# Row-tiled gate matmuls in a hybrid mLSTM / RG-LRU layer: 64x64 blocks on the two row halves of the array

## The chip, the cores and the metric

The kernel runs on one core of a Trainium2 chip. The metric is the device time of one launch in microseconds. Before the change three runs gave 1915.2, 1918.41 and 1918.58 us; their median is 1918.41 us.

## The reference, cut to what matters

The program is one layer of a diffusion backbone over 1024 latent tokens and 256 context tokens of width 2048. A modulated RMS norm feeds one wide input projection (2048 to 6160 columns). Its outputs go to two mixers: an mLSTM with 4 heads, scanned in chunks in both directions, and an RG-LRU of 1024 channels, scanned token by token in both directions. The context's final states seed the scans over the latent tokens. Both mixers' gated outputs are joined and go through an output projection (2048 to 2048), a residual and a last norm.

The RG-LRU gates are the subject here. The 1024 channels form 16 blocks of 64, and each block has its own 64x64 matrix, for two directions and two gates (r and i):

```python
xb = xc.reshape(bsz, t, R_BLOCKS, R_BLOCK)
r  = sigmoid(einsum('btgi,gij->btgj', xb, w_r).reshape(bsz, t, ch) + b_r)
ii = sigmoid(einsum('btgi,gij->btgj', xb, w_i).reshape(bsz, t, ch) + b_i)
log_a = -LRU_C * r * softplus(-lam)
a = exp(log_a)
u = sqrt(-expm1(2.0 * log_a)) * (ii * xc)      # h[t] = a[t] * h[t-1] + u[t], both directions
```

## The kernel before

All large products run in float32r, with each operand split into a high and a low part, so that a product is three matmuls (high x high, high x low, low x high). Weights come through a ring of three buffers: ScalarE copies a piece to its high part `whi` (L209), VectorE subtracts to get the low part `wlo` (L210).

The work has five stages: phase A (modulation, norm and transposes), the context projections, the heads of x with the mLSTM scans beside them, the RG phase, and the output projection. A small clock in the program (`Clock`) decides where the work of the mixers is emitted among the projections' matmuls: each mixer is a generator that sleeps for so many microseconds of projection work. The tile framework then fixes one order for each engine and waits by semaphore where data or a buffer demands it. Within an engine the order is kept.

The RG-LRU handles 128 channels at a time, "tile 0" to "tile 7", each holding two 64-channel blocks. `rg_gen` does one such tile: a convolution (POOL L663, VectorE L665), then `gate_mm`, the gate matmuls, the sigmoids (L858), the products and activations (L871 to L875), two scans (L882) and, for x, the output gate (L896). It runs twice for each tile:

- over the 256 context tokens (`ctx_rg_all`), beside the heads of x. Here the gate matmul is one plain float32 matmul (L916).
- over the 1024 latent tokens (`x_rg`), in the RG phase, beside the projections of the next tiles (`ct_unit`, lines L1176, L1179, L1182; one unit is 96 matmuls into one `mm` buffer). Here the gate matmul is the triple L1294, L1295, L1296, with xc split into `xs` (ScalarE, L1288) and `xl` (VectorE, L1289).

The two 64x64 blocks of a tile lie on the diagonal of a 128x128 matrix whose other half is zero: `load_wrg` puts them there, and the zeros are set once with a memset. For each of the 4 pairs (direction, gate) and each half of the tokens, one PSUM bank of the pool `mx` (4 banks, shared with the scans and the transposes) takes the result of 128 channels by 512 tokens, and one sigmoid of 128x512 reads it.

At the end of the RG phase stands the join with the output projection (`out_unit`, L1397 to L1399): its first block needs the two `mm` buffers, the second of which is read by the evacuation of the last z unit (ScalarE L1379, VectorE L1380). ScalarE also splits the stored outputs of the mixers there (`y_split`, L1362).

Of the kernel before, what the change touches and what calls it, by code (L numbers as in the profile page):

```python
# [9 lines left out]
F32 = mybir.dt.float32  # L10
F32R = mybir.dt.float32r
# [41 lines left out]
class Clock:  # L53
    """Emission order of the parts: each generator yields how long (in us of TensorE work) it sleeps."""
# [50 lines left out]
class Slots:  # L105
    """Counts the live tiles of one tag, so that no tile is taken before its slot's last use is emitted."""
# [26 lines left out]
class Ring:  # L133
    """Weights: loaded, split into two float32r parts, ahead of their use."""
# [14 lines left out]
    def add(self, n, cols, loads, per, dest=None):  # L149
        """n k-tiles of cols columns; loads: (first column, source [128, n, c]); per: k-tiles per piece."""  # L150
# [79 lines left out]
def tile_hymba(ctx: ExitStack, tc: tile.TileContext, x, c, cx, c_ctx, w_mod, b_mod, norm_g, w_in, b_gate,  # L230
# [63 lines left out]
    negS = const.tile([128, 16], F32, name="negS")  # L294
    hafS = const.tile([128, 16], F32, name="hafS")
# [96 lines left out]
    def wm_fill(limit=4 * KT):  # L392
        """loads of the modulation weights, as far ahead as there is room"""
# [54 lines left out]
    def mv_fin(k):  # L448
        """scale and shift columns of k-tile k: scale x, scale ctx, shift x, shift ctx"""
# [24 lines left out]
    DVE.tensor_copy(out=cols, in_=pt[:, 0:184])  # L474
    DVE.tensor_scalar(out=b1sc, in0=cols[:, cSC:cSC + 16], scalar1=1.0, scalar2=None, op0=ADD)
# [18 lines left out]
    def mv_some(n, limit):  # L494
        """the next n pieces of the modulation products"""
# [16 lines left out]
    def log1p_exp_neg(z, den, t, t2):  # L512
        """z = e^-|a| -> t(z) with log(1 + z) = 2 t(z)."""
# [10 lines left out]
    # 8 softplus(-lambda)  # L524
# [11 lines left out]
    # row norms  # L536
# [29 lines left out]
    def main_a(k, q):  # L566
        """a quarter of the products of k-tile k"""
# [17 lines left out]
    def to_hx(k, src, s, oh, ol, w, v):  # L585
        """float32r parts of scale * src + shift"""
# [56 lines left out]
    def j2r(ap):  # L643
        """[128, 1024] in raster order, seen in column-major order"""
# [16 lines left out]
    def conv(xp, cv, T, wb, bb, ct):  # L661
        """causal-style 4-tap convolution of a channel tile; xp holds T + 3 columns"""
# [862 lines left out]
```

## Time and profile before

| | |
|---|---|
| runs | 1915.2, 1918.41, 1918.58 us (median 1918.41) |
| profiled execution | span 1915.9 us from the first to the last instruction; no other time of it is given, and the span lies within the runs |
| TensorE | busy 1821.8 us, 95% |
| VectorE, ScalarE, GpSimdE | busy 930.5, 808.8 and 327.8 us |
| x gates of the RG-LRU | 192 matmuls of 512 columns, 64 sigmoids of 128x512 |
| context gates | 32 float32 matmuls of 256 columns (64 in the trace), 32 sigmoids of 128x256 |
| RG phase, first gate matmul to last sigmoid | 1194.3 to 1549.7 us |

A busy time of TensorE is not its cost in a stream: matmuls overlap in the pipeline, so that the distance from one start to the next is what each takes from the engine, and the duration (about 390 ns for 512 columns) is longer than that.

### The profile page before, as it was taken

The numbers are of one execution on the slowest core, as the hardware profiler recorded it, in microseconds if no ns is written. First come the engines' busy times: TensorE is split into PE (matmuls) and PEld (weight loads), VectorE is DVE, ScalarE is ACT, GpSimd is POOL, SyncE is SP. The second block draws the span as 40 slices with busy tenths as digits, with TensorE's granted clock in tenths as the row PEclk, the third lists the DMA queues.
The fourth block names the chain that finished last, engine by engine and source line by source line (L and its number), as shares of the span: only waits on it lengthen the run. The fifth ranks groups of instructions, "written<-read, shape, count | busy, mean of one in ns | idle before, by whom it ended". The sixth has DMA issues, their size and how long they took to land.

```text
span 1915.9 us, 24921 instructions
## 1 busy us (share of the span) xinstructions
PE 1821.8 (95%) x9489; PEld 1499.0 (78%) x9489; DVE 930.5 (49%) x1580; ACT 808.8 (42%) x1228; POOL 327.8 (17%) x414
## 2 busy tenths in 40 slices
PE   1888999999999999999999999999999989999998
PEld 0455999888898878988798878778878877888786
DVE  5776654435543552134322444777755655434432
ACT  4444553335745531133312431755555664324322
POOL 2420001012101210012000210221221223222221
PEclk9999999999999999999999999999999999999999
DMA  9996676223222132112221214344332236446533
GB/s 272 284 291 180 184 189 161 69 56 67 66 78 53 47 72 67 45 46 65 58 67 48 55 45 133 118 124 133 115 102 58 77 123 201 154 123 229 168 113 132
DMA packets 293927, 223.50 MB, mean 117 GB/s; under 512 B 25792, under 2 KB 256408, under 8 KB 293808
## 3 DMA queue, kind: packets, MB, share of 16 engines
q1 hardware_dynamic: 285688, 198.64, 37.9%
q10 hardware_dynamic: 5336, 14.36, 2.0%
q0 software_dynamic: 2784, 8.92, 1.3%
q8 instruction: 75, 1.23, 0.3%
q14 instruction: 44, 0.36, 0.1%
HBM read 202.39 MB, written 19.48 MB: 116 GB/s over the span
## 4 chain that ended last, share of the span: by engine, by line
PE 70%; DMA 9%; DVE 8%; issue 5%; ACT 4%; POOL 2%; SPq 2%; ACTq 0%; DVEq 0%; POOLq 0%
PE mm L1182 11%; PE mm L1176 11%; PE mm L1179 11%; PE mm L1219 2%; PE mm L1221 2%; PE mm L1222 2%; DMA gw<-in_w_mod_dram 2%; DMA wm<-in_w_mod_dram 2%; PE mm L1397 2%; PE mm L1398 2%; PE mm L1399 2%; PE mx L1398 2%; PE mx L1399 2%; PE mx L1397 2%; DMA yst<-yD 1%
## 5 line engine op out<-in xcount | busy, mean ns | idle before, releaser
L210 DVE TENSOR_TENSOR wlo<-raw,whi 128x512 fp32r<-128x512 f32 (+1 forms) x392 | 294.9, 761 | 562.0 <-ACT whi L209 561.4
L209 ACT ACTIVATE whi<-raw 128x512 fp32r<-128x512 f32 (+1 forms) x392 | 242.6, 628 | 559.3 <-PE mm L1179 259.0
L1176 PE MATMUL mm<-hxh,whi 128*128 128x512 f32 x1216 | 396.9, 407 | 0.3 <-DVE Gx L1208 0.3
L1182 PE MATMUL mm<-hxh,wlo 128*128 128x512 f32 x1216 | 384.4, 397 | 0.0
L1179 PE MATMUL mm<-hxl,whi 128*128 128x512 f32 x1216 | 382.6, 395 | 0.0
L1179 PEld LDWEIGHTS mm<-hxl,whi 128*128 128x128 f32 x1216 | 229.2, 188 | 54.4
L1182 PEld LDWEIGHTS mm<-hxh,wlo 128*128 128x128 f32 x1216 | 229.8, 189 | 53.3
L1176 PEld LDWEIGHTS mm<-hxh,whi 128*128 128x128 f32 x1216 | 227.6, 189 | 52.5 <-issue 1.9
L1219 PE MATMUL mm<-whi,hxh 128*128 128x256 f32 x384 | 109.8, 286 | 0.4 <-DVE s L1257 0.2
L1221 PE MATMUL mm<-wlo,hxh 128*128 128x256 f32 x384 | 108.1, 282 | 0.0
L1222 PE MATMUL mm<-whi,hxl 128*128 128x256 f32 x384 | 107.5, 281 | 0.0
L1397 PE MATMUL mm<-whi,hxh 128*128 128x512 f32 x256 | 101.8, 398 | 5.0 <-DVE s L1380 5.0
L1398 PE MATMUL mm<-wlo,hxh 128*128 128x512 f32 x256 | 101.4, 396 | 0.0
L1399 PE MATMUL mm<-whi,hxl 128*128 128x512 f32 x256 | 101.4, 396 | 0.0
L1398 PE MATMUL mx<-wlo,hxh 128*128 128x512 f32 x192 | 75.8, 395 | 2.0 <-DVE wlo L210 2.0
L1397 PE MATMUL mx<-whi,hxh 128*128 128x512 f32 x192 | 75.9, 395 | 1.7 <-ACT whi L209 1.6
L433 PE MATMUL mx<-wm,silP 128*32 128x256 f32 x512 | 43.2, 426 | 35.1 <-DMA wm<-in_w_mod_dram 30.1
L1399 PE MATMUL mx<-whi,hxl 128*128 128x512 f32 x192 | 75.5, 393 | 0.0
L1219 PEld LDWEIGHTS mm<-whi,hxh 128*128 128x128 f32 x384 | 72.5, 189 | 1.2 <-issue 0.5
L1314 DVE SCALAR_TENSOR_TENSOR ga<-gw,silc,ga 128x512 f32<-128x512 f32 x60 | 55.2, 920 | 36.4 <-DMA gw<-in_w_mod_dram 35.9
L1221 PEld LDWEIGHTS mm<-wlo,hxh 128*128 128x128 f32 x384 | 72.4, 188 | 0.3
L1222 PEld LDWEIGHTS mm<-whi,hxl 128*128 128x128 f32 x384 | 72.2, 189 | 0.0
(323 smaller groups left out, 3180.3 us busy)
## 6 DMA issues: line engine op xcount, KB each, us to landing
raw<-in_w_in_dram SPq DMA_DIRECT2D x136, 512.0 KB, 4.0
wm<-in_w_mod_dram SPq DMA_DIRECT2D x128, 256.0 KB, 5.6
raw<-in_w_out_dram SPq DMA_DIRECT2D x64, 512.0 KB, 4.8
gw<-in_w_mod_dram SPq DMA_DIRECT2D x64, 256.0 KB, 2.8
X<-in_x_dram SPq DMA_DIRECT2D x16, 512.0 KB, 7.6
NI<-niD SPq DMA_DIRECT2D x64, 128.0 KB, 4.5
xpc<-in_x_dram SPq DMA_DIRECT2D x32, 256.0 KB, 3.5
yD<-s ACTq DMA_DIRECT2D x15, 512.0 KB, 2.8
```

The lines of the kernel that those rows point to most:

```text
L209: self.nc.scalar.activation(out=hi, in_=src, func=AF.Copy)
L210: self.nc.vector.tensor_tensor(out=lo, in0=src, in1=hi.bitcast(F32), op=SUB)
L1176: PE.matmul(out=ps[:, ts], lhsT=hi, rhs=hxh[k][:, ts], start=(k == 0), stop=False)
L1179: PE.matmul(out=ps[:, ts], lhsT=hi, rhs=hxl[k][:, ts], start=False, stop=False)
L1182: PE.matmul(out=ps[:, ts], lhsT=lo, rhs=hxh[k][:, ts], start=False, stop=(k == KT - 1))
L1219: PE.matmul(out=o, lhsT=hxh[k][:, sl], rhs=hi, start=(k == 0 and tt % 2 == 0), stop=False, skip_group_check=True)
L1221: PE.matmul(out=o, lhsT=hxh[k][:, sl], rhs=lo, start=False, stop=False, skip_group_check=True)
L1222: PE.matmul(out=o, lhsT=hxl[k][:, sl], rhs=hi, start=False, stop=(k == KT - 1), skip_group_check=True)
L1314: DVE.scalar_tensor_tensor(out=a, in0=t, scalar=silc[:, k:k + 1], in1=a, op0=MUL, op1=ADD)
L1397: PE.matmul(out=pst[jt], lhsT=hxh[j][:, sl], rhs=hi, start=(j == 0), stop=False)
L1398: PE.matmul(out=pst[jt], lhsT=hxh[j][:, sl], rhs=lo, start=False, stop=False)
L1399: PE.matmul(out=pst[jt], lhsT=hxl[j][:, sl], rhs=hi, start=False, stop=(j == KT - 1))
```

## The change

The zeros are left out. The weight tile holds, for each channel of a block, the 4 x 64 columns (direction, gate, output channel), so that 128 columns of it are the r gate and the i gate of one direction. A matmul takes the 64 rows of one block and gives 128 outputs: r on partitions 0 to 63, i on partitions 64 to 127. The two blocks b of a tile stand on the two row halves of the array (`tile_position=(64 * b, 0)`), each with a PSUM bank of its own. So the number of gate matmuls is as before: 2 blocks instead of 2 gates.

A sigmoid now reads 64 partitions (one gate of one block) and writes 64 partitions, with its bias from a new small tile `brg` that four VectorE copies fill at the start. There are twice as many sigmoids. All matmuls of one direction are emitted at one point (12 for x, 2 for the context), the sigmoids behind them, and then one sleep of 3.6 us (0.9 for the context) stands in the place of the sleeps of 0.9 us after each sigmoid. The slots of both gates are taken at the start of a direction. The split of the weights (L1283, L1284) shrinks from 128x512 to 128x256, and two memsets go.

```diff
-            SP.dma_start(out=t[64 * g:64 * g + 64, :, 64 * g:64 * g + 64], in_=src)
+            SP.dma_start(out=t[64 * g:64 * g + 64, :, :], in_=src)
...
         for d in range(2):
-            for g in range(2):
-                t = yield from S.get()
-                (rt if g == 0 else it)[d] = t
-                for h0 in range(0, T, wd):
-                    ps = mx_tile()
-                    pre_g(ps[:, 0:wd], 2 * d + g, slice(h0, h0 + wd))
-                    act(out=t[:, h0:h0 + wd], in_=ps[:, 0:wd], func=AF.Sigmoid, bias=col(cBR, 8 * (2 * d + g) + i))
-                    yield 0.9
+            rt[d] = yield from S.get()
+            it[d] = yield from S.get()
+            parts = []
+            for h0 in range(0, T, wd):
+                two = [mx_tile()[:, 0:wd] for _ in range(2)]
+                pre_g(two, d, slice(h0, h0 + wd))
+                parts.append((h0, two))
+            for h0, two in parts:
+                for b in range(2):
+                    for g, t in enumerate((rt[d], it[d])):
+                        act(out=t[64 * b:64 * b + 64, h0:h0 + wd], in_=two[b][64 * g:64 * g + 64, :], func=AF.Sigmoid,
+                            bias=brg[64 * g:64 * g + 64, b, d, i:i + 1])
+            yield 3.6 * sc
...
-            def f(ps, dg, ts):
-                PE.matmul(out=ps, lhsT=W[:, dg, :], rhs=xc[:, ts], start=True, stop=True)
+            def f(two, d, ts):
+                for b, ps in enumerate(two):
+                    r = slice(64 * b, 64 * b + 64)
+                    PE.matmul(out=ps, lhsT=W[r, 2 * d:2 * d + 2, :].rearrange("p a b -> p (a b)"), rhs=xc[r, ts],
+                              start=True, stop=True, tile_position=(64 * b, 0))
...
-                PE.matmul(out=ps, lhsT=hl[:, 0, cs], rhs=xs[:, ts], start=True, stop=False)
-                PE.matmul(out=ps, lhsT=hl[:, 0, cs], rhs=xl[:, ts], start=False, stop=False)
-                PE.matmul(out=ps, lhsT=hl[:, 1, cs], rhs=xs[:, ts], start=False, stop=True)
+                for w, src in ((0, xs), (0, xl), (1, xs)):
+                    for b, ps in enumerate(two):
+                        r = slice(64 * b, 64 * b + 64)
+                        PE.matmul(out=ps, lhsT=hl[r, w, cs], rhs=src[r, ts], start=(src is xs and w == 0),
+                                  stop=(w == 1), tile_position=(64 * b, 0))
```

On TensorE, tile 4 of the RG phase shows the form that tiles 3 to 7 have. Before, the first triples stand among the projection's matmuls (`mm`), one PSUM bank (`mx`) each:

```order
L1294 MATMUL mx_11706<-s_11671,s_11616 128x512
L1295 MATMUL mx_11706<-s_11672,s_11616 128x512
L1296 MATMUL mx_11706<-s_11671,s_11616 128x512
L1176 MATMUL mm_11600<-hxh_1258,whi_11601 128x512 x2
L1179 MATMUL mm_11600<-hxl_1257,whi_11601 128x512 x2
L1182 MATMUL mm_11600<-hxh_1258,wlo_11602 128x512 x2
L1294 MATMUL mx_11718<-s_11671,s_11616 128x512
L1295 MATMUL mx_11718<-s_11672,s_11616 128x512
L1296 MATMUL mx_11718<-s_11671,s_11616 128x512
```

After, the same place holds one direction's 12 gate matmuls in a row (11768 and 11769 are the banks of the two blocks for the first 512 tokens, 11776 and 11777 for the others; 11738 and 11739 are `xs` and `xl`):

```order
L1308 MATMUL mx_11768<-s_11738,s_11680 128x512
L1308 MATMUL mx_11769<-s_11738,s_11680 128x512
L1308 MATMUL mx_11768<-s_11739,s_11680 128x512
L1308 MATMUL mx_11769<-s_11739,s_11680 128x512
L1308 MATMUL mx_11768<-s_11738,s_11680 128x512
L1308 MATMUL mx_11769<-s_11738,s_11680 128x512
L1308 MATMUL mx_11776<-s_11738,s_11680 128x512
L1308 MATMUL mx_11777<-s_11738,s_11680 128x512
L1308 MATMUL mx_11776<-s_11739,s_11680 128x512
L1308 MATMUL mx_11777<-s_11739,s_11680 128x512
L1308 MATMUL mx_11776<-s_11738,s_11680 128x512
L1308 MATMUL mx_11777<-s_11738,s_11680 128x512
```

The two halves of the array take turns there; 18 projection matmuls follow, then the 12 of the second direction. Before, a tile's eight triples were eight visits among 42 projection matmuls.

In tiles 0, 1 and 2 the second direction comes out differently on TensorE after the change (here tile 0; 10505 to 10514 are the four banks):

```order
L1308 MATMUL mx_10505<-s_10421,s_10358 128x512
L1308 MATMUL mx_10505<-s_10422,s_10358 128x512
L1308 MATMUL mx_10505<-s_10421,s_10358 128x512
L1188 MATMUL mm_10543<-hxh_529,whi_10411 128x512 x2
L1191 MATMUL mm_10543<-hxl_528,whi_10411 128x512
L1308 MATMUL mx_10506<-s_10421,s_10358 128x512
L1308 MATMUL mx_10506<-s_10422,s_10358 128x512
L1308 MATMUL mx_10506<-s_10421,s_10358 128x512
```

The three steps of one block run behind one another on one half, with projection matmuls before the other block's three. So over the eight tiles the 192 gate matmuls form 78 neighbours on opposite halves and 36 that stand alone, in 28 groups between projection matmuls; the context's 32 form 15 neighbours and 2 alone, in 14 groups.

On ScalarE, the last tile (7) and the join. Before, the last z unit's evacuation (L1379, into 12620) stands here among the sigmoids and the splits of the stored outputs (`yst`):

```order
L1362 ACTIVATE hxh_995<-yst_8_12824 128x512
L1362 ACTIVATE hxh_1083<-yst_9_12828 128x512
L858 ACTIVATE s_12797<-mx_12798,cols 128x512
L209 ACTIVATE whi_12818<-raw_12589 128x512
L1379 ACTIVATE s_12620<-mm_12621 128x64x16
L858 ACTIVATE s_12797<-mx_12809,cols 128x512
```

After, it is L1392, behind all 16 sigmoids of the tile and the same two splits:

```order
L867 ACTIVATE s_12887<-mx_12896,brg 64x512
L209 ACTIVATE whi_12928<-raw_12681 128x512
L867 ACTIVATE s_12886<-mx_12897,brg 64x512
L867 ACTIVATE s_12887<-mx_12897,brg 64x512
L1375 ACTIVATE hxh_1000<-yst_8_12934 128x512
L1375 ACTIVATE hxh_1088<-yst_9_12938 128x512
L1392 ACTIVATE s_12711<-mm_12712 128x64x16
```

What moved with it on TensorE: before, 6 matmuls of the output projection and 2 of the gates stood between the last z unit and the first use of the second `mm` buffer; after, 18 of the output projection do.

## Rows read from the trace of the kernel before

**Rows 1.** The page: busy time of each engine, share of the span, instructions.

```profile
PE 1821.8 (95%) x9489; PEld 1499.0 (78%) x9489; DVE 930.5 (49%) x1580; ACT 808.8 (42%) x1228; POOL 327.8 (17%) x414
```

**Rows 2.** Busy time by stretch: RG phase, context gates (clock and DMA last).

```profile
1194.30:1549.70 355.40, 344.19 (x1450) 275.18 (x1451) 235.18 (x221) 217.85 (x244) 82.93 (x55) 0.99 0.35 105
441.50:633.50 192.00, 191.22 (x1038) 165.00 (x1037) 85.60 (x208) 112.29 (x181) 30.02 (x67) 1.00 0.26 65
```

**Rows 3.** Timeline, TensorE: start, duration, line; gate triple, float32 matmuls of 257 columns.

```profile
1372.80 0.40 PE L1294 MATMUL mx<-s,s 128*128 128x512 f32 x1
1373.03 0.39 PE L1295 MATMUL mx<-s,s 128*128 128x512 f32 x1
...
440.04 0.60 PE L1112 MATMUL mx<-s,KW 128*128 128x257 f32 x2
...
440.48 0.60 PE L1107 MATMUL mx<-s,SP 128*128 128x257 f32 x2
```

**Rows 4.** Timeline, TensorE: modulation matmuls on four column tiles between full-array matmuls.

```profile
95.01 0.50 PE L580 MATMUL mm<-hxh,wlo 128*128 128x512 f32 x1
95.44 0.64 PE L433 MATMUL mx<-wm,silP 128*32 128x256 f32 x8
96.01 0.50 PE L577 MATMUL mm<-hxh,whi 128*128 128x512 f32 x1
...
113.22 1.07 PE L433 MATMUL mx<-wm,silP 128*32 128x256 f32 x16 [0.98 <-DVE ft L590]
```

**Rows 5.** Two stretches of 30 ns, line L433 alone (PE and PEld, count in brackets).

```profile
94.46:94.49 0.03, 0.03 (x4) 0.03 (x8) 1.00 1.22 307
94.70:94.73 0.03, 0.03 (x8) 0.00 (x0) 1.00 1.14 290
```

**Rows 6.** Timeline: matmuls of 256 columns and their weight loads (PEld).

```profile
985.03 0.28 PE L1221 MATMUL mm<-wlo,hxh 128*128 128x256 f32 x1
985.03 0.19 PEld L1222 LDWEIGHTS mm<-whi,hxl 128*128 128x128 f32 x1
985.15 0.28 PE L1222 MATMUL mm<-whi,hxl 128*128 128x256 f32 x1
```

**Rows 7.** Timeline and lines, ScalarE: sigmoids, a 64-partition copy, table loads.

```profile
1196.54 3.00 ACT L858 ACTIVATE s<-mx,cols 128x512 f32<-128x512 f32 x5 [2.22 <-PE mx L1296]
1201.20 1.85 ACT L858 ACTIVATE s<-mx,cols 128x512 f32<-128x512 f32 x3
...
L719 ACT ACTIVATE s<-mx 64x512 f32<-64x512 f32 x6 | 3.2, 588 | 3.1 <-PE mx L716 3.0
L858 ACT ACT_TABLE_LOAD x20 | 25.7, 1283 | 2.6 <-DVE gb L1323 2.2
```

**Rows 8.** Waits of TensorE from 1180 to 1620: total us, times, longest.

```profile
PE mm L1397 <- DVE s L1380: 5.0, 1, 5.0
PE mx L1294 <- ACT s L1288: 3.1, 3, 1.9
```

**Rows 9.** Timeline around tile 1: TensorE, and ScalarE's store of tile 0's output.

```profile
1236.04 0.80 PE L1294 MATMUL mx<-s,s 128*128 128x512 f32 x1 [2.08 <-ACT s L858]
1236.63 0.63 PE L1295 MATMUL mx<-s,s 128*128 128x512 f32 x1
1237.05 0.63 PE L1296 MATMUL mx<-s,s 128*128 128x512 f32 x1
...
1232.72 0.33 ACTq L904 DMA_DIRECT2D yD<-s  x1
```

**Rows 10.** The join: TensorE, ScalarE, and the stretch behind it.

```profile
1544.30 0.77 PE L1397 MATMUL mm<-whi,hxh 128*128 128x512 f32 x1 [4.96 <-DVE s L1380]
...
1537.97 1.25 ACT L1362 ACTIVATE hxh<-yst 128x512 fp32r<-128x512 f32 x2 [2.81 <-DMA yst<-yD]
1540.22 1.89 ACT L1379 ACTIVATE s<-mm 128x1024 f32<-128x1024 f32 x1
...
1545.00:1550.00 5.00, 5.00 (x14) 3.85 (x13) 1.03 (x2) 2.24 (x4) 1.38 (x3) 0.50 0.34 112
```

More of the change, by code (lines that the diff above doesn't have):

```diff
@@ L294, in tile_hymba @@
     negS = const.tile([128, 16], F32, name="negS")
+    brg = const.tile([128, 2, 2, 8], F32, name="brg")
     hafS = const.tile([128, 16], F32, name="hafS")
@@ L474, in tile_hymba @@
     DVE.tensor_copy(out=cols, in_=pt[:, 0:184])
+    for g in range(2):
+        for b in range(2):
+            DVE.tensor_copy(out=brg[64 * g:64 * g + 64, b, :, :],
+                            in_=cols[64 * b:64 * b + 64, cBR:cBR + 32].rearrange("p (d g i) -> p g d i", d=2, g=2)[:, g])
     DVE.tensor_scalar(out=b1sc, in0=cols[:, cSC:cSC + 16], scalar1=1.0, scalar2=None, op0=ADD)
@@ L851, in rg_gen @@
         for d in range(2):
-            for g in range(2):
-                t = yield from S.get()
-                (rt if g == 0 else it)[d] = t
-                for h0 in range(0, T, wd):
-                    ps = mx_tile()
-                    pre_g(ps[:, 0:wd], 2 * d + g, slice(h0, h0 + wd))
-                    act(out=t[:, h0:h0 + wd], in_=ps[:, 0:wd], func=AF.Sigmoid, bias=col(cBR, 8 * (2 * d + g) + i))
-                    yield 0.9
+            rt[d] = yield from S.get()
[6 more added lines that the diff above has]
+            for h0, two in parts:
+                for b in range(2):
+                    for g, t in enumerate((rt[d], it[d])):
+                        act(out=t[64 * b:64 * b + 64, h0:h0 + wd], in_=two[b][64 * g:64 * g + 64, :], func=AF.Sigmoid,
+                            bias=brg[64 * g:64 * g + 64, b, d, i:i + 1])
+            yield 3.6 * sc
             POOL.tensor_tensor(out=it[d][:, 0:T], in0=it[d][:, 0:T], in1=xc, op=MUL)
@@ L910, in ctx_rg_all @@
         xm, RS = env["xm"], env["RS"]
-        W = xm.tile([128, 4, 128], F32, name="cwb")
-        POOL.memset(W, 0.0)
+        W = xm.tile([128, 4, 64], F32, name="cwb")
         def gate_mm(xc):
-            def f(ps, dg, ts):
-                PE.matmul(out=ps, lhsT=W[:, dg, :], rhs=xc[:, ts], start=True, stop=True)
+            def f(two, d, ts):
[3 more added lines that the diff above has]
+                              start=True, stop=True, tile_position=(64 * b, 0))
                 clk.pe(0.43)
@@ L1269, in tile_hymba @@
     S = Slots(clk, rg, "s", SRG, [128, 1028])
-    wrg = [rg.tile([128, 4, 128], F32, name=f"xwb{i}") for i in range(1)]
-    POOL.memset(wrg[0], 0.0)
+    wrg = [rg.tile([128, 4, 64], F32, name=f"xwb{i}") for i in range(1)]
     lock = [0]
@@ L1280, in x_rg @@
         load_wrg(W, i)
-        hl = yield from S.get([128, 2, 512], F32R)
+        hl = yield from S.get([128, 2, 256], F32R)
         yield 2.0
```

4 lines of the change are left out of this document (2 added, 2 removed).

## The prediction

> **What bounds the kernel now.** I read the page's busy times first: TensorE is busy for 1821.8 of 1915.9 us [rows 1], no other engine for half of it. The next question is whether this holds in the two stretches that the change touches. In the RG phase TensorE is busy for 344.2 of 355.4 us, VectorE for 235.2, ScalarE for 217.9; in the stretch of the context gates for 191.2 of 192.0 [rows 2]. So TensorE's instruction stream is the time there: what leaves it is gained, and what another engine does costs only if TensorE waits for it. Then I looked up what each instruction takes from the stream (start to start on the timeline), how tiled matmuls behave where this kernel has some already, and where TensorE waits in the RG phase.
>
> **The gate matmuls, alone.** Two matmuls of a triple start 0.23 us apart [rows 3] (1372.80 to 1373.03; I use 0.2325, the mean over a longer stream), and 192 of them take 192 x 0.2325 = 44.6 us. The number stays; what can go is the time of one in each pair that stands on opposite halves. The instruction order has 78 such pairs and 36 matmuls that stand alone. The trace of before has no row tiles, but it has column tiles: the modulation's matmuls (L433) take 32 columns of the array each. Sixteen of them take 1.07 us and eight 0.64 [rows 4], so eight more cost 0.43 us; four of them are at work within the 30 ns from 94.46, and eight overlap in a later 30 ns [rows 5]. One stream of 256 columns takes 0.115 us (985.03 to 985.15, [rows 6]), so eight one after another would take 0.92 us: they do run abreast, and if a tile's stream is the 0.22 us of a pass in [rows 3], four of them do. Bounds for a row pair: nothing saved (the halves take turns), or one whole matmul, 0.2325 us. The nearest rows are those of column tiles, so I take the whole: 78 x 0.2325 = **-18.1 us** (0 to -18.1).
>
> **Going into tiles and out again.** The same place prices the change between full array and tiles: from the full matmul at 95.01 to the next at 96.01 are 1.00 us [rows 4], of which 0.2325 are the first matmul and 0.43 the eight tiles; 0.34 us remain for the two changes. There are 28 groups of gate matmuls between projection matmuls: 28 x 0.34 = **+9.5 us**. Bounds: nothing (a half's stream follows a full one as any other does) to 0.43 (all that is not the tiles' own stream when three of four abreast are idle at the end): 0 to +12.
>
> A weight load bears on the pair too. For matmuls of the whole array the load of the next weights starts with the running matmul (985.03 PEld beside 985.03 PE) and the next matmul follows after 0.12 us [rows 6], so a load of up to 0.19 us is hidden even behind 256 columns. By that, a pair's second step on the same half is ready when the first step's stream ends, and nothing is added.
> The Trainium skill ("TensorE: Matmul & The Clock Gate", Part 3, Packing small matmuls) says that a weight load overlaps matmuls in flight only when the row group differs. The whole-array rows above differ from that; by the rule the load on the same half would stand open in each pair, and the sum would be that of the second rival below.
>
> **ScalarE.** A sigmoid of 128x512 takes (3.00 - 1.85) / 2 = 0.575 us in a row of them, and a copy of 64x512 takes 588 ns [rows 7]: half the partitions take no less time. So 64 sigmoids more cost 64 x 0.575 = 37 us of ScalarE, which comes to 255 of 355 us in the RG phase; it has the room, on average. Whether TensorE waits is decided at each direction's burst. It needs all four `mx` banks; the second burst stands 18 projection matmuls behind the first, so the cover is 18 x 0.2325 = 4.2 us, plus 0.3 for the change of mode. The eight sigmoids of the first burst take 4.6 us, but the first two banks come free after four, and the first six matmuls need only these. A table load (1.28, [rows 7]) or a weight piece's copy (0.6, about the 588 ns above) in between takes the spare. I put 0.3 us on each of the tiles 3 to 7: **+1.5 us** (0 to +4).
>
> **The start of the RG phase.** TensorE waits for the gates' inputs three times (3.1 us, [rows 8]) and once, in tile 1, for 2.08 us on sigmoids [rows 9] that stand on ScalarE behind the store of tile 0's output (L904, 1232.72). Starts behind that wait are 0.59 and 0.42 us apart instead of 0.23, as at the lower of the clock's two levels (1.2 GHz). After the change the store stands ahead of tile 1's sigmoids too, and the 16 sigmoids of tiles 0 to 2 end 4 to 8 us later, with the evacuations (L1392) behind them; against that the first bursts of tiles 1 and 2 come 29 and 27 projection matmuls later (6.7 us). These nearly cancel: **+1 us** (-4, if tile 1's wait and its slow clock go, to +6, if one more wait of 2 us with slow clock comes in each of two tiles).
>
> **The join.** Before, L1397 waits 4.96 us: the last evacuation (L1379) starts only at 1540.22, takes 1.89, and VectorE's part ends at 1544.30, 2.2 us later; in the 5 us behind it the clock is 0.50 and 14 matmuls run where 21 would, another 1.7 us at least [rows 10]. After, the evacuation stands behind the last two sigmoids (1.15), a weight copy (0.6) and two splits (1.25): it starts about 3.0 us after the last z matmul and ends at 3.0 + 1.9 + 2.2 = 7.1. The cover is 18 output matmuls, 4.2 us. So the wait is 2.9 instead of 5.0, and the clock may hold: **-3 us** (-5 to +2).
>
> **The context.** A float32 matmul of 257 columns takes two passes, 0.44 us together [rows 3] (440.04 to 440.48). 15 pairs save 0.22 to 0.44 each (-3.3 to -6.6), 14 groups cost 0.34 each (+4.8), and the bursts may wait for banks (0 to +3): **0 us** (-2 to +4). The four copies for `brg` lie at the start beside waits for DMA and cost nothing; without that cover they would be some 0.7 us. The smaller weight split and the two memsets were hidden and gain nothing.
>
> **Sum.** -18.1 + 9.5 + 1.5 + 1 - 3 + 0 = -9.1 us against the profiled span of 1915.9, or 1906.8. The span lies 2.5 us below the median of the runs and is the only time that this execution has; laid on that median the forecast is **1909.5 us**. About 0.2%, 3.8 us, is what a measurement here tells from no change.
>
> **Rivals.**
> 1. *The halves take turns.* Then no pair saves and only the changes of mode are left: 9.5 + 4.8 for the context, + 1.5 + 1 - 3 = +13.8, **1932 us**. For it: no row of before has row tiles, in float32r or float32; the two halves stream different tokens' rows into two banks, which the column tiles (one bank, four strips) don't do. Against it: the four abreast [rows 5]. Chance 0.12.
> 2. *The weight load stands open in each pair.* The load of a half would follow the end of the matmul on that half. At the 0.115 us at which loads follow one another [rows 6] a pair saves 0.1175 instead of 0.2325: -9.1 instead of -18.1, and the sum is 0, **1918 us**. For it: a load to a half that is streaming isn't in the trace. Against it: the full array does it. This is the rule of the skill named above. Chance 0.12.
> 3. *The banks become the bound.* Place: the second burst of tiles 3 to 7. If the products' activations and a table load stand among the eight sigmoids, the banks are free 4.6 + 1.3 + 0.6 = 6.5 us after the first burst, against 4.5 of cover: 2.0 us of wait, and a wait of that length brought the lower clock in tile 1 and at the join (1.7 us each). 5 x 3.7 = +18.5 in place of +1.5: -9.1 + 17 = +7.9, **1926 us**. It decides from 3.3 us a tile on, where the gain is gone. For it: the 37 us more on ScalarE, all four banks in one hand. Against it: only two banks are needed first, and ScalarE is used at 72%. The Trainium skill ("TensorEngine Tiling (Array Packing)", PSUM Bottleneck) says that after such tiling the evacuation of PSUM may become the limit; no run of before shows it. Chance 0.12.
>
> **How the numbers follow.** The forecast has 0.64, of which some 0.04 fall within 0.2% and 0.01 beyond; rival 2 falls within 0.2% for the most part (0.11). Faster 0.60, no change 0.17, slower 0.23 (rivals 1 and 3 whole, less 0.01 where a rival is milder). With changes of mode at half the price (4.8) and the start, the join and the banks at or near their good ends (-2, -4, 0, context -1) the sum is -20, 1898 on the median; above, the range reaches to rival 3. So **1899 to 1926**; the forecast's own range is 1899 to 1915.
>
> **What would show it.** In the changed kernel's timeline two L1308 matmuls of opposite halves start within a few ns, and a group of 12 takes some 6 x 0.2325 + 0.34 = 1.7 us from the projection matmul before to the one behind; 2.8 or more would be rival 1, about 2.4 rival 2. The waits of L1308 for L867 in tiles 3 to 7 are under 1 us each; 2 us with a clock of 0.5 behind would be rival 3. L1410's wait at the join falls to about 3 us. I'm wrong if pairs save less than half a matmul, or if the 28 changes of mode take more than 0.6 us each.

## The result, and the profile after

The changed kernel takes 1953.89 us (median of 4 runs, 1948.41 to 1957.29) where the kernel before took 1918.27: ratio 1.0182, 95% interval 1.0167 to 1.0197. The forecast was 1909.5, in a range of 1899 to 1926. It is 35.6 us slower instead of 9 us faster. The profiled execution (1948.41 us) has a span of 1946.7 us, 30.8 more than before.

The projections' matmuls are the same in both kernels, so each can be paired with its twin in the other trace. The changed kernel is level with the old one until 441 us of the old (-0.2 us), 9.7 us late when the context gates are through and the RG phase begins (1172), 32.8 late at the join (1570) and 30.8 at the end. So two stretches lose, about 10 us in the context gates and 23 us in the RG phase. Windows that begin and end with the same projection matmuls show how: first before, the RG phase and the context stretch (us, then busy time and count of TensorE, weight loads, VectorE, ScalarE, GpSimdE; then the granted clock, DMA share, GB/s),

```profile
1171.87:1570.35 398.48, 386.85 (x1634) 309.41 (x1633) 260.12 (x250) 239.38 (x268) 87.78 (x63) 0.99 0.37 111
441.56:653.41 211.85, 211.07 (x1125) 181.04 (x1124) 98.00 (x231) 124.50 (x198) 34.12 (x73) 1.00 0.24 62
```

and the same two after the change:

```profile
1181.60:1603.18 421.58, 390.34 (x1634) 295.14 (x1632) 257.34 (x249) 259.67 (x313) 80.31 (x60) 0.96 0.35 104
441.40:663.88 222.48, 211.92 (x1121) 175.28 (x1120) 97.12 (x231) 135.74 (x227) 33.80 (x73) 0.98 0.22 59
```

In the RG phase TensorE stands idle for 31.2 us (421.58 - 390.34) where it was 11.6. And its busy time is 3.5 us longer although a part of the work is done in pairs: the mean clock is 0.96 instead of 0.99, by estimate 0.03 x 420 = some 12 us of slower matmuls, which hide what the pairs gain. In the context stretch idle time grows from 0.8 to 10.6 us. What TensorE waits for from 1180 to 1620 (total, times, longest), first a line of before that belongs to [rows 8], then after the change:

```profile
PE mx L1295 <- DVE s L1289: 1.5, 2, 0.8
```

```profile
PE mx L1308 <- ACT s L1299: 13.5, 4, 6.1
PE mx L1308 <- ACT s L867: 9.9, 8, 4.9
PE mx L1308 <- DVE s L1300: 3.5, 5, 0.9
PE mm L1410 <- DVE s L1393: 3.3, 1, 3.3
```

The inputs of the gates (`xs`, L1299, and `xl`, L1300) are late by 17.0 us instead of 3.1 + 1.5 = 4.6; the PSUM banks (sigmoids L867) by 9.9 instead of 2.1 [rows 9]. The join waits 3.3, against 4.96 in [rows 10].

**The pairs work.** Tile 6's first group on TensorE's timeline, the answer to [rows 3]:

```profile
1501.19 0.40 PE L1194 MATMUL mm<-hxh,wlo 128*128 128x512 f32 x1
1501.52 1.67 PE L1308 MATMUL mx<-s,s 64*128 64x512 f32 x12
1503.12 0.51 PE L1188 MATMUL mm<-hxh,whi 128*128 128x512 f32 x1
```

The single records have the two matmuls of a pair start 1 to 7 ns apart. Twelve matmuls of 512 columns take 1.60 us from the first start to the next full matmul. One by one they would take 2.79. Six pairs at 0.2325 are 1.40; 0.20 on the way out and 0.10 on the way in (1501.19 to 1501.52 less one matmul) remain for the changes of mode: 0.30 us a group, forecast 0.34. By the Trainium skill ("TensorE: Matmul & The Clock Gate", Part 3, Packing small matmuls) the weight load of a pair's second step on the same half would stand open; these rows have no room for it (six pairs with a load of 0.115 each would need 2.1 us), and the single records have the next loads of both halves start at 1501.62, 0.1 us into the first pair.

This is the only one of the ten groups of 12 in the changed kernel that runs through. Seven take 2.41 to 2.72 us, as one of tile 3 here, and each has a wait of 0.55 to 0.76 us inside, for a bank or for `xl`; such a short wait costs the group 0.8 to 1.1 us. The other two (4.02 and 6.44 us) run at the lower clock, behind waits of 4.44 and 4.88 us. That it is the waits and not the halves is seen in e3 below, where 8 of 12 such groups take 1.58 to 1.61 us; the second fence has one of them.

```profile
1349.21 1.19 PE L1308 MATMUL mx<-s,s 64*128 64x512 f32 x7
1351.02 0.96 PE L1308 MATMUL mx<-s,s 64*128 64x512 f32 x5 [0.62 <-ACT s L867]
1351.90 0.50 PE L1188 MATMUL mm<-hxh,whi 128*128 128x512 f32 x1
```

```profile
1339.30 1.66 PE L1306 MATMUL mx<-s,s 64*128 64x512 f32 x12
1340.89 0.49 PE L1186 MATMUL mm<-hxh,whi 128*128 128x512 f32 x1
```

**ScalarE's sigmoids.** ScalarE's groups for line L867, and one direction's eight sigmoids on the timeline, against [rows 7]:

```profile
L867 ACT ACTIVATE s<-mx,brg 64x512 f32<-64x512 f32 x128 | 87.4, 683 | 6.4 <-PE mx L1308 4.2
...
1252.92 5.60 ACT L867 ACTIVATE s<-mx,brg 64x512 f32<-64x512 f32 x8
```

Eight take 5.60 us, (5.60 - 0.68) / 7 = 0.70 from start to start. The forecast used the 0.575 us of 128 partitions. A tile's sigmoids now take 16 x 0.70 = 11.2 us of ScalarE instead of 8 x 0.575 = 4.6.

**Where it is lost, 1: ScalarE's order in the context.** ScalarE at the V heads' evacuation before the change (L1228), the same after it (L1240), then TensorE there after the change:

```profile
583.51 0.91 ACT L858 ACTIVATE r<-mx,cols 128x256 f32<-128x256 f32 x2 [1.28 <-PE mx L916]
585.36 1.02 ACT L1228 ACTIVATE s<-mm 128x1024 f32<-128x1024 f32 x1 [0.94 <-PE mm L1222]
...
587.31 0.46 ACT L858 ACTIVATE r<-mx,cols 128x256 f32<-128x256 f32 x1
```

```profile
591.85 1.28 ACT L881 ACT_TABLE_LOAD   x1
593.14 0.91 ACT L881 ACTIVATE r<-r,negS 128x256 f32<-128x256 f32 x2
593.96 0.61 ACT L209 ACTIVATE whi<-raw 128x512 fp32r<-128x512 f32 x1
594.47 0.89 ACT L882 ACTIVATE r<-r,hafS 128x256 f32<-128x256 f32 x2
595.38 1.28 ACT L885 ACT_TABLE_LOAD   x1
596.68 0.91 ACT L885 ACTIVATE r<-r,tiny 128x256 f32<-128x256 f32 x2
597.61 1.94 ACT L1240 ACTIVATE s<-mm 128x1024 f32<-128x1024 f32 x2
```

```profile
598.68 1.22 PE L1188 MATMUL mm<-hxh,whi 128*128 128x512 f32 x2 [5.78 <-ACT s L1240]
599.70 1.05 PE L1191 MATMUL mm<-hxl,whi 128*128 128x512 f32 x2
```

With all sigmoids of a direction at one point, the activations of the tile follow them in one run, and the evacuation that frees TensorE's buffer stands behind the run. Before, its first part stood between two sigmoids. TensorE waits 5.78 us and then runs at the lower clock: two matmuls take 1.02 us (598.68 to 599.70), at the higher clock 0.465. This is the largest part of the 10.6 us of idle time in the stretch, not all of it: TensorE also waits 2.00 us for the convolution of a context tile (VectorE L670), 1.4 us in two waits of the mLSTM's scans (L1119) and 1.07 us at L1231.

**Where it is lost, 2: the next tile's inputs.** Tile 2: VectorE with the scans of tile 1 and the convolution of tile 2, ScalarE with `xs`, and TensorE:

```profile
1278.01 4.58 DVE L892 TENSOR_TENSOR_SCAN s<-s,rini,s 128x1024 f32<-128x1024 f32 x2
1282.51 3.46 DVE L210 TENSOR_TENSOR wlo<-raw,whi 128x512 fp32r<-128x512 f32 x2
...
1291.02 1.27 DVE L670 SCALAR_TENSOR_TENSOR s<-s,cols,s 128x1024 f32<-128x1024 f32 x1
...
1292.38 1.06 ACT L1299 ACTIVATE s<-s 128x1024 fp32r<-128x1024 f32 x1 [4.19 <-DVE s L670]
...
1293.49 1.22 PE L1308 MATMUL mx<-s,s 64*128 64x512 f32 x4 [6.05 <-ACT s L1299]
```

The chain is sigmoids, activations, scans, the next tile's convolution, `xs`, the next tile's gates. From tile 0's first sigmoid to tile 1's `xs` it takes 36.0 us instead of 26.5 (1204.70 to 1240.70 on ScalarE, before 1196.54 to 1223.07), from tile 1's to tile 2's 45.7 instead of 41.7. In e3 below, with half the sigmoids, these are 26.3 and 41.0, so here it is the doubled sigmoids, with the broken order of the gates, that make the chain longer. From tile 2 on they don't do so by their own length: before, a tile's eight were spread over 17.7 us or more, and now the sixteen stand within 12.6 to 14.1. What is longer in tiles 3 to 6 is the way from the last sigmoid to the next `xs`, 33 to 38 us instead of 27 to 31. Tile 4 shows a second cause, on ScalarE and then TensorE:

```profile
1371.26 0.63 ACT L209 ACTIVATE whi<-raw 128x512 fp32r<-128x512 f32 x1 [1.82 <-PE mm L1191]
1386.28 0.33 ACTq L914 DMA_DIRECT2D yD<-s  x1
1386.71 0.63 ACT L209 ACTIVATE whi<-raw 128x512 fp32r<-128x512 f32 x1 [14.82 <-DVE s L906]
1387.25 2.01 ACT L1384 ACTIVATE s<-mm 128x1024 f32<-128x1024 f32 x1
...
1395.39 1.06 ACT L1299 ACTIVATE s<-s 128x1024 fp32r<-128x1024 f32 x1 [5.41 <-DVE s L670]
```

```profile
1396.50 0.79 PE L1308 MATMUL mx<-s,s 64*128 64x512 f32 x2 [4.44 <-ACT s L1299]
```

ScalarE does nothing for 14.8 us: the store of tile 3's output (L914) stands at the head of its queue and waits for the scans, with the evacuation of tile 4's projection (L1384) behind it. Before the change the store stood behind that evacuation in all tiles; in the new order it is in front of it for tiles 3 to 6.

**Where it is lost, 3: tile 7's banks.** ScalarE, then TensorE:

```profile
1555.76 1.21 ACT L1375 ACTIVATE hxh<-yst 128x512 fp32r<-128x512 f32 x2 [3.57 <-DMA yst<-yD]
1560.29 0.63 ACT L1375 ACTIVATE hxh<-yst 128x512 fp32r<-128x512 f32 x1 [3.31 <-DMA yst<-yD]
1560.93 1.28 ACT L867 ACT_TABLE_LOAD   x1
1562.23 1.38 ACT L867 ACTIVATE s<-mx,brg 64x512 f32<-64x512 f32 x2
```

```profile
1563.66 0.79 PE L1308 MATMUL mx<-s,s 64*128 64x512 f32 x1 [4.88 <-ACT s L867]
```

The first sigmoid begins at 1562.2, though its gates were done by 1554.4: three splits of stored outputs stand in front of it and wait for their loads. The second group needs the banks and waits 4.88 us.

### The profile page after: what moved, and what is told of

Read it like the earlier page. It is cut to its first block, busy times and chain, and to the rows that moved or that the text cites. A ratio compares the mean times of both kernels' runs of the same rounds, so it can differ in the third digit from the quotient of the medians.

```text
span 1946.7 us, 25071 instructions
## 1 busy us (share of the span) xinstructions
PE 1822.1 (94%) x9489; PEld 1477.7 (76%) x9489; DVE 925.7 (48%) x1584; ACT 841.0 (43%) x1301; POOL 321.1 (16%) x412
## 5 line engine op out<-in xcount | busy, mean ns | idle before, releaser
L210 DVE TENSOR_TENSOR wlo<-raw,whi 128x512 fp32r<-128x512 f32 (+1 forms) x392 | 289.9, 748 | 584.6 <-ACT whi L209 582.5
L1191 PE MATMUL mm<-hxl,whi 128*128 128x512 f32 x1216 | 386.8, 398 | 0.0
L1231 PE MATMUL mm<-whi,hxh 128*128 128x256 f32 x384 | 109.2, 284 | 1.2 <-DVE rini L898 1.1
L867 ACT ACTIVATE s<-mx,brg 64x512 f32<-64x512 f32 x128 | 87.4, 683 | 6.4 <-PE mx L1308 4.2
L1231 PEld LDWEIGHTS mm<-whi,hxh 128*128 128x128 f32 x384 | 72.4, 189 | 2.9 <-issue 2.4
```

What stands on the lines that cost most here:

```text
L210: self.nc.vector.tensor_tensor(out=lo, in0=src, in1=hi.bitcast(F32), op=SUB)
L867: act(out=t[64 * b:64 * b + 64, h0:h0 + wd], in_=two[b][64 * g:64 * g + 64, :], func=AF.Sigmoid, bias=brg[64 * g:64 * g + 64, b, d, i:i + 1])
L1191: PE.matmul(out=ps[:, ts], lhsT=hi, rhs=hxl[k][:, ts], start=False, stop=False)
L1231: PE.matmul(out=o, lhsT=hxh[k][:, sl], rhs=hi, start=(k == 0 and tt % 2 == 0), stop=False, skip_group_check=True)
```

## The experiments

The times are medians; the kernel before had 1919.1, 1920.0, 1922.1 and 1917.0 us beside the four sets of runs, so sets are best compared by their ratios to it.

**e1: the burst without the halves.** The program's clock also counts each gate matmul at half its time, as it does in the changed kernel (not shown here).

```diff
-            for g in range(2):
-                t = yield from S.get()
...
-                for h0 in range(0, T, wd):
-                    ps = mx_tile()
-                    pre_g(ps[:, 0:wd], 2 * d + g, slice(h0, h0 + wd))
-                    act(out=t[:, h0:h0 + wd], in_=ps[:, 0:wd], func=AF.Sigmoid, bias=col(cBR, 8 * (2 * d + g) + i))
-                    yield 0.9
...
+            for h0 in range(0, T, wd):
+                two = [mx_tile()[:, 0:wd] for _ in range(2)]
+                for g in range(2):
+                    pre_g(two[g], 2 * d + g, slice(h0, h0 + wd))
+                parts.append((h0, two))
+            for h0, two in parts:
+                for g, t in enumerate((rt[d], it[d])):
+                    act(out=t[:, h0:h0 + wd], in_=two[g], func=AF.Sigmoid, bias=col(cBR, 8 * (2 * d + g) + i))
+            yield 3.6 * sc
```

> The full 128x128 weights with zeros and sigmoids of 128x512 as before, but emitted as after the change: all 12 matmuls of a direction at one point, four banks, then the four sigmoids, one sleep. Theory S (the doubled ScalarE work decides: in the changed kernel 64x512 sigmoids start 0.70 us apart where 128x512 ones start 0.575 apart, so a tile has 16 x 0.70 = 11.2 us of them instead of 4.6, and xs of the next tile and the banks come late): this kernel has the old ScalarE work, so its time is within 8 us of before, 1914 to 1926. Theory O (the burst decides: all gates first, then all sigmoids, so the chain from sigmoids to scans to the next tile's convolution starts late): most of the loss is here too, 1940 to 1960. Theory M (the row halves themselves cost TensorE time): 1914 to 1922.

Measured: 1944.04 us (1940.74 to 1946.89), ratio 1.0142 (1.0116 to 1.0168). Theory O holds, S alone and M fall: 25 us are lost with the old matmuls and the old sigmoids. In its trace the RG phase begins 10.3 us late, as much as in the changed kernel, and the store stands in front of the next evacuation as well, for tiles 2 to 6.

**e2: halves without the burst.**

```diff
-            parts = []
             for h0 in range(0, T, wd):
                 two = [mx_tile()[:, 0:wd] for _ in range(2)]
                 pre_g(two, d, slice(h0, h0 + wd))
-                parts.append((h0, two))
-            for h0, two in parts:
                 for b in range(2):
                     for g, t in enumerate((rt[d], it[d])):
...
-            yield 3.6 * sc
+                yield 1.8
```

> Row halves and 64-partition sigmoids as after the change, but each direction emitted in two parts (6 matmuls into two banks, 4 sigmoids, a sleep of 1.8 us), close to the spread of before. Theory O: the loss goes and the pairs are gained, 1905 to 1918. Theory S: the doubled sigmoids are all still there, 1938 to 1955. Theory M: 1940 to 1955.

Measured: 1935.25 us, ratio 1.0101 (1.0072 to 1.0131). Between the two theories: 15 us by the ratios (18.6 by the times) come back, and about half of the loss stays.

**e3: the changed kernel with half the sigmoids.**

```diff
-                for b in range(2):
-                    for g, t in enumerate((rt[d], it[d])):
-                        act(out=t[64 * b:64 * b + 64, h0:h0 + wd], in_=two[b][64 * g:64 * g + 64, :], func=AF.Sigmoid,
-                            bias=brg[64 * g:64 * g + 64, b, d, i:i + 1])
+                for b, t in enumerate((rt[d], it[d])):
+                    act(out=t[:, h0:h0 + wd], in_=two[b], func=AF.Sigmoid, bias=brg[:, b, d, i:i + 1])
```

> The changed kernel with its bursts and its row halves, but each PSUM bank is read by one sigmoid of 128x512 that writes 128 partitions of one tile; the gates so land on the wrong channels, and the output is not the reference's. The instruction order of TensorE is that of the kernel with zeros in bursts for tiles 3 to 7. Theory S: the loss goes and the pairs stay: 1900 to 1915, and below the kernel with zeros in bursts by 78 to 96 pairs x 0.2325 less 0.3 us for each change of mode, some 10 to 15 us. Theory O: 1925 to 1945. Theory M: as slow as the changed kernel, 1945 to 1957.

Measured: 1934.71 us, ratio 1.0093 (1.0067 to 1.0119). This is 9.3 us below e1, from the same set of runs, with the same order in tiles 3 to 7: the gain of the halves. It may not be held against the forecast's 18.1 - 9.5 = 8.6, since e3's order has 93 pairs in 18 groups and not 78 in 28; the same prices give 93 x 0.2325 - 18 x 0.30 = 16 us there, and 10 to 15 were expected. And it is 0.9% (17 us) below the changed kernel: the price of sixteen sigmoids instead of eight, with the broken order of tiles 0 to 2 that goes with them (15 pairs less and 10 groups more, by the same prices 6.5 us). The RG windows between the same projection matmuls, e1 and then e3, have it too:

```profile
1182.14:1593.09 410.95, 390.99 (x1634) 311.46 (x1632) 264.63 (x250) 216.72 (x251) 79.26 (x63) 0.98 0.35 107
```

```profile
1181.86:1582.29 400.43, 380.00 (x1634) 293.83 (x1632) 260.62 (x250) 212.40 (x251) 83.78 (x62) 0.97 0.37 110
```

TensorE's idle time is 20 us in both; its busy time is 11 us less with the halves, at a mean clock of 0.97 instead of 0.98 (by estimate 0.01 x 400 = 4 us). The longest wait on `xs` is 3.5 us in e3, against 6.1 in the changed kernel:

```profile
PE mx L1306 <- ACT s L1297: 8.3, 4, 3.5
```

Theories S and O so are two halves of one account. In ratios: burst +1.42%, halves -0.49%, doubled sigmoids +0.89%, together the +1.82% of the changed kernel; in us about +27, -9 and +17. Steps that are taken one after another always add up like this, but the RG windows allow a test, with e2 as the fourth kernel (409.8 us between the same matmuls). There the burst costs 12.5 us (e1 against before) or 11.8 (the changed kernel against e2), the halves gain 10.5, the doubled sigmoids cost 21.2; the halves and the doubled sigmoids without the burst, e2 against before, cost 11.3, close to 21.2 - 10.5. The context's loss belongs to the burst alone: e1, e2 and e3 begin the RG phase 10.3, 10.4 and 10.0 us late, whatever their matmuls and sigmoids (in e2 too a context direction is emitted at one point, since it has only one part).

**e4: halves for the latent tokens alone.** The context keeps the zeros, the matmuls and the sigmoids of before (`if ini:` around the new loop, the old one in its `else`).

> Row halves for the latent tokens as after the change; the 256 context tokens keep the zeros, 32 matmuls and 32 sigmoids of before and their order. In the trace of the changed kernel the projections' matmuls are 9.7 us later than before when the RG phase begins, and 21 us more are lost in the RG phase. If the two losses add, this kernel takes 1938 to 1946; if the loss before the RG phase is given back by slack in the RG phase, 1948 to 1957.

Measured: 1945.39 us, ratio 1.0151 (1.0126 to 1.0177). The two losses add; the context's is 8.5 us by the times and 6 by the ratios. In its trace the context stretch loses nothing (0.9 us late at its start, 0.8 at its end), and the RG window takes 420.2 us, nearly the 421.6 of the changed kernel.

**e5: the order of the sigmoids.**

```diff
-            for h0, two in parts:
-                for b in range(2):
-                    for g, t in enumerate((rt[d], it[d])):
+            for b in range(2):
+                for g, t in enumerate((rt[d], it[d])):
+                    for h0, two in parts:
```

> The changed kernel with the eight sigmoids of a direction in another order: the two halves of the tokens of one (block, gate) stand behind one another, so every second step keeps the partitions that it reads and writes. In the changed kernel all 94 steps between neighbouring 64x512 sigmoids are 0.69 to 0.71 us, where 128x512 ones without a wait start 0.57 apart. Theory P (the step from one set of partitions to another ends the overlap of neighbours): every second step falls to about 0.57. Theory H (64 partitions alone do it): all stay at 0.70. The time, a single one, should lie within 1945 to 1960 either way.

Measured: 1948.95 us (one run). Told apart by the order of ScalarE's instructions, the steps between neighbouring sigmoids in the RG phase are these: of 45 that keep the partitions, 39 are now 0.59 us (three more are 0.69 or 0.70, three wait); of 62 that change them, all are 0.68 to 0.71. In the changed kernel all 107 change them, at 0.69 to 0.71. Fewer than every second step keep them, since the order that was fixed for ScalarE has some of the old neighbours again. Seven in a row on ScalarE's timeline:

```profile
1252.80 4.52 ACT L867 ACTIVATE s<-mx,brg 64x512 f32<-64x512 f32 x7 [0.17 <-PE mx L1308]
```

(4.52 - 0.68) / 6 = 0.64, the mean of 0.59 and 0.70. Theory P holds: a step to other partitions costs 0.11 us more.

**e6: context as before, spread halves for the latent tokens** (e4 with the loop of e2).

> Context as before the change; latent tokens on row halves, each direction in two parts (6 matmuls, 4 sigmoids, a sleep of 1.8 us). If the loss in the stretch of the context gates (9.7 to 10.4 us in all three kernels that burst or tile there) and that of the RG phase add, this is 10 us under the spread kernel: 1922 to 1929, still slower than before by the waits of the RG phase. If the RG phase swallows it, 1932 to 1940.

Measured: 1928.90 us, ratio 1.0054 (1.0036 to 1.0072). As expected; with e14 below the best of the versions with halves in all tiles, and still slower than before. The longest wait that remains is tile 2's (tile 7 waits 4.6 us for its banks):

```profile
1279.52 1.22 PE L1316 MATMUL mx<-s,s 64*128 64x512 f32 x4 [7.69 <-ACT s L1307]
```

**e7: evacuations first.** One number: `evac=60` for `evac=0`.

> The changed kernel with one number altered: the evacuations of the projections' PSUM buffers have a higher priority (60 instead of 0), so that on ScalarE the evacuation of the V heads stands in front of the tanh and square roots of a context tile, and that of the last z unit in front of two sigmoids and two splits. The theory that TensorE's wait of 5.8 us on the V heads' evacuation and of 3.3 us at the join are ScalarE's order alone: about 4 and 2.6 us of them go, and with them some of the low clock behind each: 1943 to 1949. Rival (ScalarE is simply full there, the place does not matter): 1950 to 1957.

Measured: 1945.88 us, ratio 1.0132 (1.0106 to 1.0159), 8 us less than the changed kernel (9.6 by the ratios). On ScalarE, then TensorE:

```profile
595.09 1.02 ACT L1240 ACTIVATE s<-mm 128x1024 f32<-128x1024 f32 x1
...
597.43 0.50 ACT L882 ACTIVATE r<-r,hafS 128x256 f32<-128x256 f32 x1
```

```profile
596.16 0.73 PE L1188 MATMUL mm<-hxh,whi 128*128 128x512 f32 x2 [1.85 <-ACT s L1240]
```

The evacuation has passed the tile's tanh and square roots, and the wait is 1.85 instead of 5.78; that at the join is 1.6 instead of 3.3. For these waits ScalarE was not full, it was in the wrong order. The two traces don't show the gain as a whole: their executions took 1948.57 and 1948.41 us, where the medians are 1945.88 and 1953.89, and the RG phase still begins 9.0 us late instead of 9.7.

**e8: the gates later in TensorE's order.** `yield 11.0` for `yield 5.0` behind the split of xc.

> The changed kernel with the gates of each latent tile 24 projection matmuls (5.6 us) later in TensorE's order: the sleep between the split of xc and the first gates is 11 us instead of 5. Theory of place (TensorE meets the gates before their input is there; the tile's chain of sigmoids, activations, scans and the next convolution has room): the waits on xs and xl (17 us in 9) and half the low clock behind them go, 1925 to 1938. Theory of the cycle (the chain of one tile ends in the next tile's gates, and is longer than a tile's matmuls): the waits come back behind later gates and at the join, 1945 to 1960.

Measured: 1947.84 us, ratio 1.0154 (1.0131 to 1.0178). The theory of the cycle holds. The waits, 1180 to 1620:

```profile
PE mx L1308 <- ACT s L867: 16.2, 8, 10.2
PE mx L1308 <- ACT s L1299: 7.7, 1, 7.7
```

Tiles 4 and 7 no longer wait for `xs`, but tile 2 now waits 7.7 us, and the banks of tile 7 now come 10.2 us late. A wait put off comes back at the end of the chain.

**e9 and e10: halves in some tiles.** The kernel before, with the spread halves of e2 in tiles 2 to 6 (e9) or 3 to 6 (e10); the zeros everywhere else.

```diff
+        if ini and i in RG_ORDER[2:7]:
...
+                    two = [mx_tile() for _ in range(2)]
+                    pre_g(two, d, slice(h0, h0 + wd))
...
+                    yield 1.8
...
+        else:
...
```

> The kernel before, with row halves in tiles 2 to 6 of the latent tokens alone, each direction in two parts; tiles 0, 1 and 7 and the context keep the zeros and the 128x512 sigmoids. A tile on row halves saves 12 pairs x 0.2325 = 2.8 us and pays 4 changes of mode of 0.30: 1.6 us. In the kernel with the context of before and the spread gates, tiles 3 to 6 waited 0.3 to 1.4 us each for their inputs and tile 2 waited 7.7. Theory (the longer sigmoids cost only where a tile's chain has no room, which is tile 2 behind two tiles on row halves, and tile 7): 5 x 1.6 = 8 us less than before, less some small waits: 1910 to 1916 where before has 1918 to 1920. Rival (every tile on row halves makes the next one late): 1920 to 1930.

> The same with row halves in tiles 3 to 6 alone. Theory: 4 x 1.6 = 6.4 us less than before, less small waits: 1911 to 1917; if tile 2 on row halves is what costs, this one is the faster of the two. Rival: 1919 to 1927.

Measured: 1928.96 us, ratio 1.0044 (1.0030 to 1.0059), and 1927.37, ratio 1.0027 (1.0013 to 1.0041). My theory that tiles 3 to 6 have room is wrong; e9 lies in the rival's range and e10 0.4 us above it. In both kernels tile 5 waits for `xs` (4.7 and 5.0 us) and runs at the lower clock behind, and the gain of the pairs is gone. (These kernels also split a tile's weights in two copies of 64 partitions; no run tells what this costs.) In e10's trace ScalarE had stood for 16.6 us before that, with the store in front of the evacuation, which led to the next four.

**e11 to e14: the store on GpSimd.** One word in the changed kernel (e11), in e9 (e12), in the kernel before as the control (e13), in e6 (e14):

```diff
-                ACT.dma_start(out=yD[8 + i], in_=y)
+                POOL.dma_start(out=yD[8 + i], in_=y)
```

> The changed kernel with one word altered: the store of a tile's output (yD) is issued by GpSimd instead of ScalarE. In the changed kernel's order this store stands in front of the next tile's evacuation (L1384) on ScalarE for tiles 3 to 6, and ScalarE waits there 11 to 17 us for the scans; before, it stood behind that evacuation in all tiles. Theory Q (the store's new place in ScalarE's queue makes the gates' inputs of tiles 4 to 7 late): tile 4's wait of 4.9 us with its low clock and part of tile 7's go: 1938 to 1947. Rival (the chain through sigmoids and scans is late by itself): 1949 to 1957. Tile 2's wait of 6.1 us is not touched by either.

> Row halves in tiles 2 to 6, the rest as before, and the store on GpSimd. In the two hybrids tile 5 waited 5 us behind ScalarE's wait of 16.6 us at the store. Theory Q: that wait and its low clock go (5 + 5 us): 1915 to 1921, level with before or below it. Rival: 1925 to 1932.

> The kernel before with the store on GpSimd alone, as the control for the other three: there the store makes only tile 1's sigmoids wait (2.1 us and a low clock of 3.4 us behind). Theory Q: 0 to 4 us less than before. Rival (GpSimd's queue then delays the convolutions): up to 5 us more.

> Context as before, latent tokens on row halves in two parts per direction, and the store on GpSimd. Against the same kernel with the store on ScalarE (1928.9, where tile 2 waits 7.7 us and tile 7's second half 4.6): in that one the later tiles waited only 0.3 to 1.4 us, so theory Q gives little, 1923 to 1929; the waits of tile 2 and tile 7 stay.

Measured: e11 1944.60 us, ratio 1.0159 (1.0127 to 1.0190); e12 1923.82, 1.0040 (1.0022 to 1.0057); e13 1920.22, 1.0021 (1.0003 to 1.0039); e14 1927.76, 1.0066 (1.0041 to 1.0091). e11's tile 4, ScalarE and then TensorE:

```profile
1379.96 2.02 ACT L1384 ACTIVATE s<-mm 128x1024 f32<-128x1024 f32 x1
...
1394.79 1.06 ACT L1299 ACTIVATE s<-s 128x1024 fp32r<-128x1024 f32 x1 [9.16 <-DVE s L670]
```

```profile
1395.90 0.50 PE L1308 MATMUL mx<-s,s 64*128 64x512 f32 x2 [1.25 <-ACT s L1299]
```

The block on ScalarE is gone and the wait falls from 4.44 to 1.25 us. But `xs` now waits for VectorE, whose convolution comes after tile 3's scans: behind the queue stands the chain. Against the expectation, in e14 the waits of tiles 2 and 7 fall too, from 7.7 and 4.6 us to 4.5 and 1.9. Tile 5's wait falls likewise, from 4.7 us in e9 to 2.1 in e12.

In total time theory Q is not borne out, nor quite refuted: e11 and e14 lie in its ranges, e12 between the two, e13 in the rival's. By the ratios e11's interval overlaps that of the changed kernel, e12 is no faster against its own runs of before than e9, and the control is 0.2% slower. Measured against the control, whose store is on GpSimd too, the change costs 1.3% in e11 instead of 1.8 and the halves 0.2% in e12 instead of 0.4. So the store's place is a part of it, of some 3 us of wait in one or two tiles of a kernel, and not the cause of the whole.

No version with row halves beats the kernel before. That the splits in front of tile 7's sigmoids cost the 4.88 us there was read from the trace alone; no run took them away.

## Why the prediction was wrong

In the RG phase the forecast's terms come to -9.1 us and the windows show +23.1. Of the 32 us between them, 19.6 are new idle time of TensorE and some 12 are matmuls at the lower clock (busy time +3.5 us where the pairs should have brought -8.6). Another 9.9 us come from the context, where the forecast had 0.

**The pairs and the changes of mode (-18.1 and +9.5): right as prices.** 12 matmuls take 1.60 us where nothing is waited for, a group costs 0.30 us, and the halves gain 9.3 us between e1 and e3. In the changed kernel most of it is lost again, by the 0.8 to 1.1 us that a short wait costs in each of seven groups and by the lower clock. Rivals 1 and 2 are out.

**ScalarE (+1.5): the step that failed.** "Whether TensorE waits is decided at each direction's burst." For the banks this held nearly: the second bursts of tiles 3 to 6 wait some 0.6 us each, for 0.3 forecast. But the time is decided a link further on. The sigmoids begin a chain that ends in the next tile's inputs, and behind the start of the RG phase the prediction has no term for its length, nor anywhere one for collecting a direction's sigmoids at one point; both stood at nothing without a reason. The next tile's `xs` and `xl` came late (17.0 us in 9 waits against 4.6), and the long waits among them brought the lower clock. In the RG phase the burst alone, with the old matmuls and sigmoids, costs 12.5 us (e1), and the doubled sigmoids, 0.70 us each where 0.575 was taken, cost 21.2 (the changed kernel against e3, with the broken order of tiles 0 to 2). By which link each later tile is held up was read from the trace and in part argued. The Trainium skill's warning ("TensorEngine Tiling (Array Packing)", PSUM Bottleneck) that reading PSUM may become the limit behind a faster TensorE holds here in part: the banks are waited for 9.9 us, the inputs that come after them 17.0. A share of 72% for ScalarE said nothing on this.

**The start of the RG phase (+1): wrong.** I let the later sigmoids and the later first bursts cancel. Tile 2's gates do stand 27 matmuls later, but its inputs stand behind tile 1's chain, which moved with them: 6.05 us of wait and a clock below 1 behind it (the stretch from 1293.5 to 1303.5 has a mean of 0.68). The projections' matmuls are 9.7 us late at 1172 of the old trace and 20.2 at 1300. e8 shows that moving the gates still later only hands the wait on.

**The join (-3): right in its place, and paid elsewhere.** The wait is 3.3 us, forecast 2.9. But tile 7's second burst, just ahead of it, now waits 4.88 us.

**The context (0): wrong, +9.9.** I counted matmuls and banks there. The largest single wait, 5.78 of 10.6 us, comes from the place of the V heads' evacuation in ScalarE's queue, which the burst moved. e4 puts 6 to 8.5 us on the context; e7 takes 8 us back with the priority alone, though its trace shows only the two shorter waits of it, 3.9 us there and 1.7 at the join.

**The order.** It showed the store in front of the evacuation in tiles 3 to 6 before anything ran; I looked at tile 1's only. e11 puts it at some 3 us of tile 4's wait.

**Rival 3** had the right engine and the wrong place: of the second bursts only tile 7's waits long for banks (4.88 us), and the longest waits of tiles 2 and 4 are for `xs`, at their beginning (6.05 and 4.44 us). Its 1926 us was 28 short, since it left out the context and the chain. (By its own sum the gain is gone from 10.6 / 5 = 2.1 us a tile on, not from 3.3.)

## What to carry to other kernels

Count an engine's added work along the chain that it is a link of, not as a share of its time: where one tile's last result is the next tile's first input, what lengthens a tile's chain counts once its slack is used up. Price the collecting of instructions as a change of its own: here it cost more (25 us in e1, with the old matmuls and sigmoids) than the new matmuls gained. When a change gathers instructions in one place, read each in-order queue for what now stands in front of the instructions that free a buffer or feed the next stage. Halving a matmul is worth little if it doubles the instructions that read its result.

## What was new of the hardware

Two row halves of 64 in float32r run side by side into two PSUM banks, at one matmul's pace for a pair (0.23 us for 512 columns), and going into them and out again costs 0.30 us. A wait of 0.6 us inside such a group costs it 0.8 to 1.1. A sigmoid of 64x512 costs ScalarE more than one of 128x512 (0.70 against 0.57 us from start to start) if its neighbours use other partitions, and 0.59 if they use the same.
